# Projections and modulation vectors moved inside two attention blocks of a two-layer transformer stack

## The chip, the cores and the metric

The kernel runs on one core of a Trainium2 chip. The metric is device time in microseconds (us), lower is better. Before the change three runs took 2095.98, 2098.3 and 2098.57 us, the median being 2098.3 us. Products of TensorE (PE) are in fp32 pieces; VectorE is DVE, ScalarE is ACT, GpSimd is POOL, and SP issues most weight transfers.

## The reference, cut to what matters

Input x is 512 tokens by 1024 features. Four blocks follow one another; each begins with an RMS norm that is scaled and shifted by vectors computed from a conditioning row c:

```python
mod = silu(c) @ w_ada[layer] + b_ada[layer]          # three rows of 1024: shift, scale, gate
h = rmsnorm(x, g_pre) * (1 + scale) + shift
# block 1 (even): z = h @ w_in, split into latent q and kv (MLA, 8 heads), SWA q, k, v (8 heads, window 128), gate
o = concat([mla(...), swa_sink(...)]) * silu(z_gate);  x = x + gate * rmsnorm(o @ w_out)
# block 2 (odd): z = h @ w_in, split into dq, dk, dv (4 differential heads), fq, fk, fv, ff (8 forgetting heads), gate
o = concat([diff(...), forgetting(...)]) * silu(z_gate);  x = x + gate * rmsnorm(o @ w_out)
# then a convolution block with an MLP, an HGRN2 block with an MLP, and a last RMS norm
```

All attention is causal (SWA over a band of two blocks), softmax is in fp32, and every product with a weight matrix must keep fp32 accuracy.

## The kernel before, in words

**Products.** Every fp32 operand of a large product is split into a high and a low half of a reduced fp32 type, and `mm3` (L206) issues three TensorE instructions for each pair of 128-row tiles (high by high, low by high, high by low). `wgran` (L210) brings a granule of 512 KB of a weight matrix to a `raw` buffer by SP, casts the high half on ACT (L222) and subtracts to get the low half on DVE or, every `lo_pool`-th time, on POOL (L225). Five `hl` buffers hold granules. `gemm_xs` (L288) takes tokens as the stationary operand: for each of four token blocks it accumulates 8 x 3 products into one PSUM buffer and hands it to an `evac` function. `gemm_ws` (L351) takes the weights as stationary operand and gives transposed results, 512 tokens wide. PSUM tags are `mm`, `sc`, `tp` with two buffers each, `pv` and `tq` with one.

**Attention.** The generators `mla`, `swa`, `diff` and `fox` each have 16 steps (head pairs, or heads, by four query blocks). A step is scores (PE), a masked minimum (DVE, L633), an exponential (ACT, L635), a reciprocal (DVE, L636), a scaling (POOL, L640), transposes of the probabilities (PE, L663), a copy (ACT, L665) and products with V (PE, L682 or L673). Queries and keys of `mla`, `swa` and `diff` go through DRAM: the projection's evac applies the rotary embedding (two DVE operations L619 and L621, one POOL addition L622), ACT issues a store, and `load` reads a head back and transposes it through PSUM tag `tq` (`heads_T`, L646 to L653).

**Weaving.** `weave` (L263) takes one step of an attention generator and then as many units of a `fill` generator as a cost function allows. A unit is one k-step of a 512-wide product group (three products). `behind` ties the fill to the PE instruction of six steps earlier, so fill may run at most about six steps ahead. The source order gives priorities; a planner with a timeline of its own puts each engine's instructions in a fixed order, so an engine's queue runs strictly in that order on the chip.

**Even block.** After the latent projections the kernel runs the SWA queries' projection (columns 672 to 1183, `gemm_x(..., ev_sq)`) and the first gate alone, then the latent up-projections, then weaves `mla` with 52 units of fill and `swa` with 24: gates 1 to 3, SWA keys and values, gates 4, 6, 5, 7.

**Odd block.** The projections dq, dk and dv, each 512 wide, run alone; then comes the small `ff` product, then `diff` woven with 80 units (gates 0 to 5 and fv), then the first pair of `fqk` alone, then `fox` woven with 64 units (three pairs of `fqk`, gates 6 and 7).

**Vectors.** `ada` makes the modulation rows for later blocks. Each row is eight steps, appended to `pend`, and `tick` runs one after a product group. `step` (L531) issues an SP load into one of two `araw` buffers and adds it up with two DVE operations (L540, L542); the last of four sums partitions with eight small products (L548). `step_pe` (L512) does the same by eight small TensorE products (L522) and one DVE addition (L524), one tick after the load. Only the convolution block uses `step_pe` before the change. Even and odd blocks have four rows, 32 steps, each.

Of the kernel before, what the change touches and what calls it, by code (L numbers as in the profile page):

```python
# [16 lines left out]
P = 128  # L17
D = 1024
T = 512
NTB = T // P  # L20
KC = D // P
# [9 lines left out]
C_CH = C_SM + 256  # L31
C_SH = C_CH + 256
# [7 lines left out]
STRICT = 0  # L40
FD = 6
ADA_OFF = 0
W_MLA = 52
ONDVE = (0, 1, 2)
W_FOX = 3
MAIN_OFF = 0
# [13 lines left out]
TV = 0  # L60
TVE = 3
# [3 lines left out]
SQF = 0  # L65
G0 = 2
ADA_LAG = 1
# [45 lines left out]
class K:  # L113
# [174 lines left out]
    def gemm_xs(self, act, w, c0, cw, kc, evac, tag="mm", subs=None):  # L288

        gs = self.wload(w, c0, cw, kc)  # L290
        subs = subs or [(0, cw)]
        for tb in range(NTB):
            outs = []
            for s0, sw in subs:
                ps = self.psum(("mm", "sc")[tb % 2] if len(subs) > 1 else tag)
                for k in range(kc):
                    g, j = gs[k]
                    self.mm3(ps[:, :sw], [a[:, k, tb * P:(tb + 1) * P] for a in act],
                             [g[:, a, j, s0:s0 + sw] for a in range(2)], k == 0, k == kc - 1, TERMS_R)
# [185 lines left out]
    def ada(self, ccol, w, b, c0, kind, g=None):  # L485
# [45 lines left out]
        def step(half, gk):  # L531
            if gk == 0:
                st[half] = self.rp.tile([P, 512], F32, tag="acc", name=self.nm("acc"), bufs=1)
            acc = st[half]
            raw = load(half, gk)
            for k in range(2):
                c = ccol[:, gk * 2 + k:gk * 2 + k + 1]
                eng = nc.gpsimd if half in self.ada_pool else nc.vector
                if gk + k == 0:
                    eng.tensor_scalar(out=acc, in0=raw[:, k], scalar1=c, scalar2=None, op0=ALU.mult)  # L540
                else:
                    eng.scalar_tensor_tensor(out=acc, in0=raw[:, k], scalar=c, in1=acc, op0=ALU.mult, op1=ALU.add)  # L542
# [218 lines left out]
    def even(self, act, gs):  # L761
# [43 lines left out]
            nc.scalar.dma_start(out=sqd[tb * P:(tb + 1) * P, 8:10, :], in_=t.rearrange("p (n d) -> p n d", d=64))  # L805
            nc.scalar.copy(out=SV[:, tb], in_=ps[:, 128:256])

        if TV == 1:
            self.tick_every = TVE
        o = self.otile()  # L810
        if SQF:
            self.run(self.gates(act, w, 1440, o, (0, 1)[:G0]))
        else:
            self.gemm_x(act, w, 672, 512, KC, ev_sq)
        if TV == 2:
            self.tick_every = TVE
        cT = [self.b4() for _ in range(5)]
        for c in range(5):
            ps = self.psum("tp")
# [92 lines left out]
                self.pv_out(o[:, 4 + hd // 2, :], pv)  # L912

        def fill():
            if SQF:
                yield from self.gates(act, w, 1440, o, (0, 1)[G0:])
                yield from self.gemm_xs(act, w, 1184, 256, KC, ev_sk)
                yield from self.gates(act, w, 1440, o, (2,))
                yield from self.gemm_xs(act, w, 672, 512, KC, ev_sq)
                yield from self.gates(act, w, 1440, o, (3, 4, 6, 5, 7))  # L920
                return
            yield from self.gates(act, w, 1440, o, (1, 2, 3))
            yield from self.gemm_xs(act, w, 1184, 256, KC, ev_sk)
            yield from self.gates(act, w, 1440, o, (4, 6, 5, 7))

        self.lo_pool = LOP[0]
        if not SQF:
            self.run(self.gates(act, w, 1440, o, (0,)))
        g = fill()
        self.weave(mla(), 16, g, W_MLA + 16 * SQF)  # L930
        self.weave(swa(), 16, g, (96 - 8 * G0 if SQF else 76) - W_MLA)
        return o


    def odd(self, act):
# [2 lines left out]
        dqk = self.dp.tile([T, 2, 512], F32, name="dqk")  # L938
        lam_init = 0.8 - 0.6 * math.exp(-0.3 * 1)

        def ev_rope(i):
            def e(tb, ps):
                t = self.tmp()[:, :512]
                self.rope(t.rearrange("p (n d) -> p n d", d=64), ps.rearrange("p (n d) -> p n d", d=64), tb, 8, 64, C_CH, C_SH)
                nc.scalar.dma_start(out=dqk[tb * P:(tb + 1) * P, i, :], in_=t)
            return e

        def ev_v(V):
# [17 lines left out]
        sub = self.cp.tile([P, 1], F32, name="sub")  # L966
        nc.vector.tensor_scalar(out=sub, in0=self.vcol("od_subln", 0), scalar1=0.5 * (1.0 - lam_init), scalar2=None, op0=ALU.mult)

        self.gemm_x(act, w, 0, 512, KC, ev_rope(0))
        self.gemm_x(act, w, 512, 512, KC, ev_rope(1))  # L970
        V = []

        def ev_vd(tb, ps):
            V.append(self.work("Vd", [P, 512]))
            nc.scalar.copy(out=V[tb], in_=ps)

        self.gemm_x(act, w, 1024, 512, KC, ev_vd)
        o = self.otile()

        A = self.work("foxA", [P, T], F32R)  # L980
# [91 lines left out]
        V2, qkT = [], {}  # L1072

        def fill():
            yield from self.gates(act, w, 3080, o, range(6))
            yield from self.gemm_xs(act, w, 2560, 512, KC, ev_v(V2))

        self.lo_pool = LOP[1]
        self.weave(diff(), 16, fill(), 80)
        self.run(fqk(0, qkT))  # L1080

        def fill():
            for p in range(1, 4):
                yield from fqk(p, qkT)
                if p > 1:
                    yield from self.gates(act, w, 3080, o, (p + 4,))

        g = fill()
        main = fox(qkT, V2)
        self.weave(main, 16, g, lambda i: min(4 * i, 16) + max(0, min(5 * (i - 4), 40)) + max(0, 2 * (i - 12)))  # L1090
        self.run(g)
        return o

# [547 lines left out]
def build(tc, h, upto=99):  # L1641
    nc = tc.nc
    with ExitStack() as es:
# [17 lines left out]
        def first(i, mixer, act, xsrc, xdst, wout, **bufs):  # L1661
            with tc.tile_pool(name="xp", bufs=1, reuse_waits="tile") as k.xp:
                with k.scope(**bufs):
                    k.tick_every = TO if i else 1000
                    k.ada_pool = AP[i]
                    rows = [k.ada(cc, wa[i], ba[i], 2048, "gatepost", h["g_post"][i])]
                    if i == 0:
                        rows += [k.ada(cc, wa[1], ba[1], 1024, "scale", h["g_pre"][1]),
                                 k.ada(cc, wa[1], ba[1], 0, "shift")]
                    else:  # L1670
                        rows += [k.ada(cc2, wa2[0], ba2[0], 1024, "scale", h["norm1_g_2"][0]),
                                 k.ada(cc2, wa2[0], ba2[0], 0, "shift")]
                        mods[0] = [k.ada(cc2, wa2[0], ba2[0], 2048, "gate")]
                    if G2 == 2 + i:
                        mods["g2"] = k.ada(cc2, wa2[0], ba2[0], 5120, "gate")
                    o = mixer(act)
                    k.flush()
                    k.lo_pool, k.tick_every = 0, 1
                    k.ada_pool = ()
                    if MK & 4:  # L1680
                        k.mark()
                with k.scope(t4=3, rows=3, oT=2, hl2=3):
# [145 lines left out]
```

## Time and profile before

| | before |
|---|---|
| median of three runs | 2098.3 us |
| profiled execution: time / span | 2094.94 / 2093.2 us |
| PE busy | 1956.3 us (93%) |
| weight loads (PEld) busy | 1585.6 us (76%) |
| DVE / ACT / POOL busy | 64% / 41% / 35% |
| mean granted TensorE clock | 0.963 |

The span is the stretch from the first to the last instruction; the profiled execution's own time is 1.7 us longer. A PE that is listed as busy is not PE at its peak: ends of products are modelled, and short gaps disappear. The granted clock is 1.00 at 2.4 GHz and 0.50 at 1.2 GHz. The even block lies at about 30 to 360 us of the span, the odd block at about 360 to 760 us.

### The profile page before, as it was taken

How to read it: one execution, taken by the hardware profiler on the slowest of the kernel's cores; microseconds unless marked ns; L12 is line 12 of the kernel's file. 1: busy time of each engine (PE TensorE's matmuls, PEld its weight loads, DVE VectorE, ACT ScalarE, POOL GpSimd, SP SyncE). 2: the span in 40 equal slices, each digit the busy share in tenths (PEclk: the TensorE clock that was granted, in tenths of full speed). 3: DMA queues.
4: the chain of work that ended last, by engine and by line, in shares of the span. 5: the costliest groups of instructions: out<-in, count | busy, mean ns of one | idle time of the engine just before them, and what ended most of it. 6: DMA issues, size and time to landing. Idle time of an engine off the chain costs nothing.

```text
span 2093.2 us, 32588 instructions
## 1 busy us (share of the span) xinstructions
PE 1956.3 (93%) x12759; PEld 1585.6 (76%) x12759; DVE 1345.0 (64%) x1979; ACT 861.8 (41%) x1461; POOL 733.1 (35%) x660
## 2 busy tenths in 40 slices
PE   7799999798999999879899999999999998999998
PEld 5688668565667787458788989877877778898896
DVE  5356775535545479547987748667786858485673
ACT  4345553133554432143434435343554534353452
POOL 1233334221233333015232331456675544223232
PEclk9999979997999999899999999999999999999999
DMA  8484655277343436832554225453322322242331
GB/s 311 129 230 136 180 166 161 80 164 145 80 97 104 149 117 187 223 99 71 178 178 153 87 75 182 134 152 103 103 83 82 121 83 80 91 131 71 121 102 60
DMA packets 225745, 272.09 MB, mean 130 GB/s; under 512 B 26682, under 2 KB 145689, under 8 KB 225592
## 3 DMA queue, kind: packets, MB, share of 16 engines
q1 hardware_dynamic: 188982, 232.83, 37.8%
q10 hardware_dynamic: 36610, 37.18, 5.9%
q8 instruction: 101, 1.65, 0.3%
q14 instruction: 52, 0.43, 0.1%
HBM read 253.57 MB, written 16.40 MB: 129 GB/s over the span
## 4 chain that ended last, share of the span: by engine, by line
PE 41%; DVE 12%; issue 4%; DMA 4%; POOL 2%; ACT 1%; ACTq 0%; SPq 0%; POOLq 0%; DVEq 0%
PE mm L208 23%; PE mm L1223 4%; PE sc L208 4%; PE sc L1223 3%; PE tp L1223 3%; DVE acc L542 2%; DVE ol L1343 2%; DVE hl L201 1%; DMA ud<-u 1%; DVE hl L225 1%; DMA raw<-in_ada_w_dram 1%; PE pv L208 1%; DVE X L1585 1%; DMA u<-ud 1%; DMA raw<-in_mlp_w_dram 0%
## 5 line engine op out<-in xcount | busy, mean ns | idle before, releaser
L208 PE MATMUL mm<-hTh,hl 128*128 128x512 f32 (+2 forms) x1200 | 375.3, 389 | 3.0 <-DVE V L201 1.5
L222 ACT CAST hl<-raw 128x1024 fp32r<-128x1024 f32 (+2 forms) x219 | 224.4, 1033 | 245.7 <-PE mm L208 142.8
L208 PE MATMUL mm<-hl,hid 128*128 128x512 f32 x1344 | 316.9, 395 | 4.9 <-DVE hid L201 3.3
L225 DVE TENSOR_TENSOR hl<-raw,hl 128x1024 fp32r<-128x1024 f32 (+2 forms) x190 | 251.0, 1331 | 78.3 <-ACT hl L222 77.8
L208 PEld LDWEIGHTS mm<-hl,hid 128*128 128x128 f32 x1344 | 251.9, 188 | 64.7 <-DVE hid L201 4.3
L208 PEld LDWEIGHTS mm<-hTh,hl 128*128 128x128 f32 (+1 forms) x1200 | 221.6, 191 | 51.6 <-issue 3.8
L208 PE MATMUL mm<-hl,hTh 128*128 128x512 f32 (+3 forms) x752 | 223.6, 375 | 26.5 <-DVE t L621 11.0
L208 PE MATMUL mm<-hTl,hl 128*128 128x512 f32 (+2 forms) x600 | 232.8, 388 | 0.1
L1140 POOL TENSOR_TENSOR xr<-xr,t 128x512 f32<-128x512 f32 x56 | 80.3, 1433 | 305.6 <-DVE t L1137 304.2
L208 PEld LDWEIGHTS mm<-hl,hTh 128*128 128x128 f32 x752 | 141.8, 199 | 52.2 <-ACT t L788 8.7
L542 DVE SCALAR_TENSOR_TENSOR acc<-araw,ccol,acc 128x512 f32<-128x512 f32 x154 | 135.0, 876 | 36.3 <-DMA araw<-in_ada_w_dram 24.3
L640 POOL TENSOR_TENSOR s<-s,sm 128x256 f32<-128x256 f32 (+3 forms) x112 | 82.8, 740 | 193.1 <-DVE sm L636 184.9
L200 ACT CAST hl<-raw 128x1024 fp32r<-128x1024 f32 x84 | 86.8, 1048 | 135.9 <-PE mm L208 111.3
L208 PE MATMUL mm<-hl,hTl 128*128 128x512 f32 (+3 forms) x376 | 139.8, 372 | 0.4 <-DVE hTl L458 0.4
L201 DVE TENSOR_TENSOR hl<-raw,hl 128x1024 fp32r<-128x1024 f32 x84 | 131.3, 1578 | 13.6 <-ACT hl L200 12.9
L208 PEld LDWEIGHTS mm<-hTl,hl 128*128 128x128 f32 (+1 forms) x600 | 114.5, 191 | 23.6 <-issue 2.0
L1203 POOL TENSOR_TENSOR raw<-raw,raw 128x1024 f32<-128x1024 f32 x28 | 76.2, 2722 | 144.4 <-DVE rows L1203 95.1
L225 POOL TENSOR_TENSOR hl<-raw,hl 128x1024 fp32r<-128x1024 f32 x29 | 73.1, 2520 | 120.5 <-ACT hl L222 120.5
L635 ACT ACTIVATE s<-s,sm 128x256 f32<-128x256 f32 (+5 forms) x128 | 69.6, 544 | 95.0 <-DVE sm L633 89.4
L1137 DVE TENSOR_TENSOR t<-mm,rows 128x512 f32<-128x512 f32 x56 | 38.5, 687 | 106.8 <-PE mm L208 103.1
L208 PE MATMUL sc<-b,b 64*128 64x256 f32 (+7 forms) x384 | 94.5, 361 | 10.5 <-DVE sm L633 8.2
L1588 POOL TENSOR_TENSOR X<-X,T 128x512 f32<-128x512 f32 x56 | 74.2, 1330 | 50.5 <-ACT op L1548 32.7
(366 smaller groups left out, 3960.4 us busy)
## 6 DMA issues: line engine op xcount, KB each, us to landing
raw<-in_mlp_w_dram SPq DMA_DIRECT2D x128, 512.0 KB
araw<-in_ada_w_dram SPq DMA_DIRECT2D x72, 512.0 KB
raw<-in_hgrn_w_in_dram SPq DMA_DIRECT2D x40, 512.0 KB
araw<-in_w_ada_dram SPq DMA_DIRECT2D x32, 512.0 KB
raw<-in_od_w_in_dram SPq DMA_DIRECT2D x32, 512.0 KB
raw<-in_ada_w_dram SPq DMA_DIRECT2D x24, 512.0 KB
rows<-row SPq DMA_DIRECT2D x16, 512.0 KB
raw<-in_conv_w_in_dram SPq DMA_DIRECT2D x16, 512.0 KB
```

What stands on the lines that cost most here:

```text
L200: nc.scalar.copy(out=hi, in_=src)
L201: nc.vector.tensor_tensor(out=lo, in0=src, in1=hi.bitcast(F32), op=ALU.subtract)
L208: self.nc.tensor.matmul(out, lhsT=lt[a], rhs=rt[b], start=start and n == 0, stop=stop and n == 2)
L222: self.nc.scalar.copy(out=hi, in_=raw[:, :n])
L225: eng.tensor_tensor(out=lo, in0=raw[:, :n], in1=hi.bitcast(F32), op=ALU.subtract)
L542: eng.scalar_tensor_tensor(out=acc, in0=raw[:, k], scalar=c, in1=acc, op0=ALU.mult, op1=ALU.add)
L635: nc.scalar.activation(out=s[:, :m], in_=s[:, :m], func=AF.Exp, scale=-1.0, bias=mn, accum_out=sm)
L640: nc.gpsimd.tensor_tensor(out=p, in0=p, in1=r.to_broadcast([P, n]), op=ALU.mult)
L1140: eng.tensor_tensor(out=xs, in0=xs, in1=t, op=ALU.add)
L1203: eng.tensor_tensor(out=out, in0=x, in1=y, op=f)
L1223: nc.tensor.matmul(ps[:, m * 256:m * 256 + 256], lhsT=ws[n][:, a, k, m * P:m * P + P], rhs=parts[n][b][:, k], start=m + k + t == 0, stop=m ...
L1588: nc.gpsimd.tensor_tensor(out=xk, in0=xk, in1=cap(Tt, 1, [(row - 1, 2), (2, nb), (0, hh)]), op=ALU.mult)
```

## The change

In the even block the SWA queries' projection leaves the front and becomes part of the fill, and so does gate 0; `mla` is woven with 80 units and `swa` with 32, 112 in all (76 before). The 32 vector steps of this block use `step_pe`, through PSUM tag `tq`. In the odd block dq, dk and dv are projected in two halves of 256 columns: heads 0 and 1 before `diff`, through `mm` and `sc` buffers in turn, heads 2 and 3 inside `diff`'s fill. `diff` has 128 units of fill (gate 0, the second halves, gates 1 and 2, fv, gate 3, the first pair of `fqk`), `fox` has 80 at six a step. Everywhere, `step` does its DVE sums one tick after its load.

```diff
-W_MLA = 52
+W_MLA = 80
@@ gemm_xs
-                ps = self.psum(("mm", "sc")[tb % 2] if len(subs) > 1 else tag)
+                ps = self.psum(("mm", "sc")[tb % 2] if len(subs) > 1 or tag == "wide" else tag)
@@ ada, step
             raw = load(half, gk)
+            self.ada_late.append(lambda: sums(half, gk, acc, raw))
+            self.ada_do(ADA_LAG)
+
+        def sums(half, gk, acc, raw):
             for k in range(2):
@@ even
-            self.gemm_x(act, w, 672, 512, KC, ev_sq)
...
-            yield from self.gates(act, w, 1440, o, (1, 2, 3))
+            yield from self.gates(act, w, 1440, o, (0,))
             yield from self.gemm_xs(act, w, 1184, 256, KC, ev_sk)
-            yield from self.gates(act, w, 1440, o, (4, 6, 5, 7))
+            yield from self.gates(act, w, 1440, o, (1, 2))
+            yield from self.gemm_xs(act, w, 672, 512, KC, ev_sq)
+            yield from self.gates(act, w, 1440, o, (3, 4, 6, 5, 7))
-            self.run(self.gates(act, w, 1440, o, (0,)))
-        self.weave(mla(), 16, g, W_MLA + 16 * SQF)
-        self.weave(swa(), 16, g, (96 - 8 * G0 if SQF else 76) - W_MLA)
+        self.weave(mla(), 16, g, W_MLA)
+        self.weave(swa(), 16, g, 112 - W_MLA)
@@ odd
-        self.gemm_x(act, w, 0, 512, KC, ev_rope(0))
-        self.gemm_x(act, w, 512, 512, KC, ev_rope(1))
-        self.gemm_x(act, w, 1024, 512, KC, ev_vd)
+        def dqkv(n):
+            for i in range(2):
+                yield from self.gemm_xs(act, w, 512 * i + 256 * n, 256, KC, ev_rope(i, 256 * n), tag="wide" if n == 0 else "mm")
+            yield from self.gemm_xs(act, w, 1024 + 256 * n, 256, KC, ev_vd(256 * n), tag="wide" if n == 0 else "mm")
+        self.run(dqkv(0))
...
-            yield from self.gates(act, w, 3080, o, range(6))
+            yield from self.gates(act, w, 3080, o, (0,))
+            yield from dqkv(1)
+            yield from self.gates(act, w, 3080, o, (1, 2))
             yield from self.gemm_xs(act, w, 2560, 512, KC, ev_v(V2))
-        self.weave(diff(), 16, fill(), 80)
-        self.run(fqk(0, qkT))
+            yield from self.gates(act, w, 3080, o, (3,))
+            yield from fqk(0, qkT)
             for p in range(1, 4):
                 yield from fqk(p, qkT)
-                if p > 1:
-                    yield from self.gates(act, w, 3080, o, (p + 4,))
+                yield from self.gates(act, w, 3080, o, (p + 3,))
+            yield from self.gates(act, w, 3080, o, (7,))
-        self.weave(main, 16, g, lambda i: min(4 * i, 16) + max(0, min(5 * (i - 4), 40)) + max(0, 2 * (i - 12)))
+        self.weave(diff(), 16, g, lambda i: 8 * i)
+        self.weave(fox(qkT, V2), 16, g, lambda i: 6 * i)
@@ first
+                    k.ada_pe, k.ada_ps = i == 0, "tq"
```

`ev_rope` and `ev_vd` are cut to 256 columns accordingly: twice as many rotary operations, stores and copies, each half as wide.

## Rows read from the trace of the kernel before

**Rows 1.** Windows: us; busy PE, PEld, DVE, ACT, POOL (count); clock, DMA, GB/s.
```profile
145.00:163.00 18.00, 15.49 (x84) 12.59 (x83) 13.85 (x32) 8.24 (x20) 5.56 (x6) 0.82 0.73 224
163.00:280.00 117.00, 114.25 (x776) 85.98 (x775) 84.55 (x234) 62.83 (x173) 42.95 (x75) 1.00 0.50 144
280.00:307.30 27.30, 27.30 (x119) 17.26 (x118) 17.08 (x53) 11.28 (x38) 10.64 (x21) 0.51 0.58 167
...
370.00:463.00 93.00, 79.42 (x332) 60.02 (x332) 41.63 (x61) 24.50 (x30) 23.87 (x15) 0.94 0.54 126
463.00:535.00 72.00, 59.39 (x248) 42.74 (x249) 37.79 (x98) 26.19 (x58) 13.54 (x12) 0.76 0.63 121
535.00:592.00 57.00, 54.84 (x267) 39.08 (x266) 31.63 (x83) 30.94 (x61) 15.19 (x12) 1.00 0.52 106
592.00:682.00 90.00, 89.83 (x477) 64.22 (x478) 44.93 (x123) 41.57 (x99) 32.77 (x35) 0.96 0.32 98
682.00:699.60 17.60, 15.65 (x112) 9.90 (x110) 7.50 (x22) 10.13 (x26) 5.36 (x7) 1.00 0.52 169
699.60:2093.00 1393.40, 1322.36 (x9297) 1104.77 (x9296) 965.61 (x1118) 564.46 (x809) 520.76 (x397) 0.98 0.38 118
```

**Rows 2.** Timeline of PE, 512-wide products: start, length, line, operation, count.
```profile
84.97 0.39 PE L208 MATMUL mm<-hl,hTl 128*128 128x512 f32 x1
...
88.47 0.40 PE L208 MATMUL mm<-hl,hTl 128*128 128x512 f32 x1
88.71 0.51 PE L208 MATMUL sc<-hl,b 128*128 128x384 f32 x2
```

**Rows 3.** Timeline of PE, 256-wide products in latent attention's fill.
```profile
181.11 0.27 PE L208 MATMUL mm<-hl,hTl 128*128 128x256 f32 x1
...
182.53 0.28 PE L208 MATMUL mm<-hl,hTl 128*128 128x256 f32 x1
```

**Rows 4.** Groups of DVE, 145 to 307 us: busy, mean ns, idle before.
```profile
L542 DVE SCALAR_TENSOR_TENSOR acc<-araw,ccol,acc 128x512 f32<-128x512 f32 x56 | 47.4, 847 | 1.6 <-DMA araw<-in_ada_w_dram 1.4
```

**Rows 5.** Timeline of PE, vector products of both kinds.
```profile
803.45 1.08 PE L522 MATMUL tp<-araw,ccol 128*32 128x128 f32 x32
804.46 0.50 PE L208 MATMUL mm<-hTl,hl 128*128 128x512 f32 x1
...
686.86 0.43 PE L548 MATMUL mm<-acc,ones 128*32 128x128 f32 x8
687.22 0.79 PE L208 MATMUL sc<-b,b 64*128 64x384 f32 x3
```

**Rows 6.** Line L524, 760 to 1000 us: ns min/median/max, first and last start.
```profile
L524 DVE TENSOR_TENSOR arow<-tp,arow x16: 271/274/279, 788.9 to 846.3; 128x128 f32<-128x128 f32 x16
```

**Rows 7.** Timeline of PE, last product of the even block's fill.
```profile
273.46 0.39 PE L208 MATMUL mm<-hTh,hl 128*128 128x512 f32 x1
```

**Rows 8.** Waits for buffer araw, 395 to 545 us: us, times; then DVE's timeline, idle in brackets.
```profile
  DMA araw<-in_ada_w_dram: 11.0, 3
...
505.44 0.75 DVE L542 SCALAR_TENSOR_TENSOR acc<-araw,ccol,acc 128x512 f32<-128x512 f32 x1 [3.74 <-DMA araw<-in_ada_w_dram]
```

**Rows 9.** Timeline of PE in differential attention.
```profile
506.51 1.01 PE L208 MATMUL sc<-b,b 64*128 64x256 f32 x3 [3.45 <-DVE sm L633]
```

**Rows 10.** Timeline of all engines, start of the odd block.
```profile
391.48 0.33 ACTq L945 DMA_DIRECT2D dqk<-t  x1
391.92 1.99 ACT L222 CAST hl<-raw 128x1024 fp32r<-128x1024 f32 x2 [11.64 <-POOL t L622]
```

**Rows 11.** Groups of DVE, 360 to 470 us.
```profile
L619 DVE TENSOR_TENSOR ru<-mm,cst 128x512 f32<-128x512 f32 x8 | 5.5, 689 | 9.8 <-PE mm L208 8.6 <-POOL t L622 1.2
```

**Rows 12.** Timeline of PE, last product of the odd block's fill.
```profile
682.69 0.40 PE L208 MATMUL mm<-hTh,hl 128*128 128x512 f32 x1
```

**Rows 13.** Waits: line L522, 760 to 1000 us; then DVE, 1340 to 1640 us.
```profile
  DVE ol L1343: 9.9, 9
...
DVE acc L542 <- DMA raw<-in_ada_w_dram: 19.6, 7, 4.7
```

More of the change, by code (lines that the diff above doesn't have):

```diff
@@ L806, in ev_sk @@
             nc.scalar.copy(out=SV[:, tb], in_=ps[:, 128:256])
-        if TV == 1:
-            self.tick_every = TVE
         o = self.otile()
-        if SQF:
-            self.run(self.gates(act, w, 1440, o, (0, 1)[:G0]))
-        else:
-            self.gemm_x(act, w, 672, 512, KC, ev_sq)
-        if TV == 2:
-            self.tick_every = TVE
         cT = [self.b4() for _ in range(5)]
@@ L914, in fill @@
         def fill():
[L915 to L921, printed above, removed]
-            yield from self.gates(act, w, 1440, o, (1, 2, 3))
+            yield from self.gates(act, w, 1440, o, (0,))
             yield from self.gemm_xs(act, w, 1184, 256, KC, ev_sk)
-            yield from self.gates(act, w, 1440, o, (4, 6, 5, 7))
+            yield from self.gates(act, w, 1440, o, (1, 2))
+            yield from self.gemm_xs(act, w, 672, 512, KC, ev_sq)
+            yield from self.gates(act, w, 1440, o, (3, 4, 6, 5, 7))
         self.lo_pool = LOP[0]
-        if not SQF:
-            self.run(self.gates(act, w, 1440, o, (0,)))
         g = fill()
-        self.weave(mla(), 16, g, W_MLA + 16 * SQF)
-        self.weave(swa(), 16, g, (96 - 8 * G0 if SQF else 76) - W_MLA)
+        self.weave(mla(), 16, g, W_MLA)
+        self.weave(swa(), 16, g, 112 - W_MLA)
         return o
@@ L939, in odd, with ev_rope @@
         lam_init = 0.8 - 0.6 * math.exp(-0.3 * 1)
-        def ev_rope(i):
+        def ev_rope(i, c):
             def e(tb, ps):
-                t = self.tmp()[:, :512]
-                self.rope(t.rearrange("p (n d) -> p n d", d=64), ps.rearrange("p (n d) -> p n d", d=64), tb, 8, 64, C_CH, C_SH)
-                nc.scalar.dma_start(out=dqk[tb * P:(tb + 1) * P, i, :], in_=t)
+                t = self.tmp()[:, :256]
+                self.rope(t.rearrange("p (n d) -> p n d", d=64), ps[:, :256].rearrange("p (n d) -> p n d", d=64), tb, 4, 64, C_CH, C_SH)
+                nc.scalar.dma_start(out=dqk[tb * P:(tb + 1) * P, i, c:c + 256], in_=t)
             return e
@@ L967, in odd, with ev_vd, e @@
         nc.vector.tensor_scalar(out=sub, in0=self.vcol("od_subln", 0), scalar1=0.5 * (1.0 - lam_init), scalar2=None, op0=ALU.mult)
-        self.gemm_x(act, w, 0, 512, KC, ev_rope(0))
-        self.gemm_x(act, w, 512, 512, KC, ev_rope(1))
[L971 to L975, printed above, removed]
-        self.gemm_x(act, w, 1024, 512, KC, ev_vd)
+        V = [self.work("Vd", [P, 512]) for _ in range(NTB)]
+        def ev_vd(c):
+            def e(tb, ps):
+                nc.scalar.copy(out=V[tb][:, c:c + 256], in_=ps[:, :256])
+            return e
+        def dqkv(n):
[3 more added lines that the diff above has]
+        self.run(dqkv(0))
         o = self.otile()
@@ L1074, in fill @@
         def fill():
-            yield from self.gates(act, w, 3080, o, range(6))
+            yield from self.gates(act, w, 3080, o, (0,))
+            yield from dqkv(1)
+            yield from self.gates(act, w, 3080, o, (1, 2))
             yield from self.gemm_xs(act, w, 2560, 512, KC, ev_v(V2))
-        self.lo_pool = LOP[1]
-        self.weave(diff(), 16, fill(), 80)
-        self.run(fqk(0, qkT))
-        def fill():
+            yield from self.gates(act, w, 3080, o, (3,))
+            yield from fqk(0, qkT)
             for p in range(1, 4):
                 yield from fqk(p, qkT)
-                if p > 1:
-                    yield from self.gates(act, w, 3080, o, (p + 4,))
+                yield from self.gates(act, w, 3080, o, (p + 3,))
+            yield from self.gates(act, w, 3080, o, (7,))
+        self.lo_pool = LOP[1]
         g = fill()
-        main = fox(qkT, V2)
-        self.weave(main, 16, g, lambda i: min(4 * i, 16) + max(0, min(5 * (i - 4), 40)) + max(0, 2 * (i - 12)))
+        self.weave(diff(), 16, g, lambda i: 8 * i)
+        self.weave(fox(qkT, V2), 16, g, lambda i: 6 * i)
         self.run(g)
@@ L1679, in first @@
                     k.ada_pool = ()
+                    k.ada_pe = False
                     if MK & 4:
```

## The prediction, as it was put on record

> **What bounds the kernel now.** I read the page's busy times first, then windows by stage, then the timelines of PE and DVE in the stretches that the change touches. The chain of waits was no help, since its listing begins only at the convolution block, behind both attention blocks.
>
> PE is listed as busy for 93% of the span, but that hides two losses: idle time, and busy time at a clock below 1.00. I add them per stretch as (length − PE busy) + PE busy × (1 − clock). In the even block [rows 1] this gives 2.5 + 2.8 = 5.3 us for 145 to 163 us (the beginning of latent attention), 2.8 us for 163 to 280, and 13.4 us for 280 to 307.3, where PE is listed as busy throughout, but at clock 0.51 (all but a moment of it at 1.2 GHz). Sum 21.5 us. In the odd block [rows 1] the front, 370 to 463 us, loses 13.6 + 4.8 = 18.4 us; differential attention loses 12.6 + 14.3 = 26.9 us (463 to 535), 2.2 us (535 to 592) and, with the beginning of forgetting attention, 3.8 us (592 to 682), together 32.9 us; the end of forgetting attention loses 2.0 us. So PE is the bound of both blocks, with about 75 us of it not used. Moving a product from one dense place to another gains nothing; it gains what it fills of these losses.
>
> DVE is not the bound, though it is a link of each step: between 163 and 280 us it is busy for 84.6 of 117 us [rows 1], and 47.4 us of its time from 145 to 307 us are vector sums [rows 4]. PE waits through it where a sum stands in DVE's queue in front of a softmax and its weights have not come: three such waits, 11.0 us in all [rows 8]; behind the one of 3.74 us PE stands for 3.45 us, until a reciprocal in DVE's queue is through [rows 9].
>
> **The even block, part by part.** *SWA queries.* 96 products of 512 columns. Fifteen stand between 84.97 and 88.47 us [rows 2], so one takes 0.233 us at the full clock and the projection 22.4 us. They leave the front and come back as 32 units of fill, net 0 on PE. Their casts, rotary work and stores move with them, under attention in which ACT (62.8 of 117 us) and POOL (43.0) have room [rows 1]. What is late next is the latent up-projection: its first product came at 88.71 us, between products of the SWA queries [rows 2]. From 84 us PE now has little else, since the three granules of that weight and two of the next take all five buffers, and gate 0 comes behind them. Cost 0 to 4.7 us; I take 3, nearer to the row.
>
> *Vectors on TensorE.* 32 steps of eight products. In the convolution block 32 products take 803.45 to 804.46, 1.01 us [rows 5], so the 256 take 8.1 us in such batches. Alone between other work, eight narrow products take 0.36 us [rows 5], which gives 32 × 0.36 = 11.5 us. The eight groups of partition sums go, 8 × 0.36 = 2.9 us. So +5.2 to +8.6 us on PE; I take +7, since ticks come singly here. DVE loses 47.4 us of sums [rows 4] and gains 32 additions of 0.274 us [rows 6], 8.8 us. That is 38.6 us less on an engine that is not the bound, worth only what comes next. The price of a product that waits for `tq` is the second rival.
>
> *Beginning of latent attention.* DVE is busy for 13.9 of the 18 us in which PE loses 5.3 [rows 1]. With the sums gone I take back 3; the bounds are 0 and 5.3.
>
> *End of SWA.* The fill's last product starts at 273.46 us [rows 7], 33.8 us before the end. After the 52 units of latent attention, 20 of the 72 real units were left, at 1.5 a step: they were used up, as the source counts, at step 13.3. Now 32 units at 2 a step last to step 16. That covers 2.7 steps more; a step without fill takes about 4 us (27.3 us hold 53 DVE operations, some eight a step, so 6.5 steps), so 11 of the 33.8 us and about a third of the 13.4 us: −4.4. The bounds are 0, if the planner puts the fill as far ahead as before relative to its end, and −13.4.
>
> Sum for the even block: 3 + 7 − 3 − 4.4 = **+2.6 us**. Its order by itself gains nothing that its vectors don't cost.
>
> **The odd block, part by part.** *Halves.* 288 products of 512 columns become 576 of 256. From 181.11 to 182.53 us there are twelve 256-wide ones [rows 3], 0.1183 us each: 68.2 us against 67.2, +1.0. Each brings its own weight load, and the row's pitch has it in it. The Trainium skill (TensorE: Matmul & The Clock Gate, LDWEIGHTS (loading the stationary operand)) speaks against the halves: a load takes its columns divided by 1.2 GHz, 107 ns for 128. By that page's figure 288 more loads would add 31 us, an estimate, if nothing hid them; the row says that the products do hide them.
>
> Rotary operations double in number at half the width. A DVE one took 0.689 us for 512 columns [rows 11]; in halves the sixteen pairs cost between nothing more and, at full price each, 11 us more of DVE in 90 us. DVE is busy for under half of the front and 37.8 of 72 us behind it [rows 1], so this is hidden; without that cover it would delay a store, not PE, since a half of `diff` needs only its own heads. ACT's stores rise by eight issues of 0.33 us [rows 10], behind which its casts stand in the same queue; 2.6 us, hidden by the four granules on hand.
>
> *The stall in the front.* A rotary addition on POOL is late, ACT's store at 391.48 us waits for it, and two casts wait behind that store; ACT has sat 11.64 us [rows 10]. The constants that POOL and DVE compute ahead of it don't change, so I keep this loss: 0.
>
> *Differential attention.* 33.7 us of projection move from before it into its fill, with the first `fqk` pair; gates 4 and 5 go to `fox`. Fill per step rises from 5 units, 3.5 us, to 8 units, 5.6 us. A softmax that is 3 to 4 us late now finds that much more queued ahead of the product that needs it. The lag of one tick also takes a sum whose load has just been issued out of the softmax's way. It doesn't help a burst of ticks: there are still two `araw` buffers, each held a tick longer. Of the 32.9 us lost here I take back 20: the 11 us of waits and the clock that falls after them (14.3 us), less a fifth. The bounds are 0 and 32.9.
>
> *Forgetting attention.* 80 units at 6 a step end at step 13.3, where 64 were spread to step 16. Before, the last fill came at 682.69 us [rows 12], with 17 us left, in which 2.0 us were lost at the full clock [rows 1]. Now about 18 us more have no fill. By that row +2; if the clock falls there as at the end of SWA, 0.49 × 18 = +9. I take +3.
>
> Sum for the odd block: 1 − 20 + 3 = **−16 us**.
>
> **The lag elsewhere.** DVE waits for vector loads for 19.6 us in the HGRN block [rows 13], but behind the odd block PE is idle for 71 of 1393 us at clock 0.98 [rows 1], in four blocks of work. There the loads share the four `raw` buffers with the weights, and the lag holds one longer. Bounds −10 and +3; I take −2.
>
> **Sum.** 2.6 − 16 − 2 = −15.4 us, from the profiled execution's 2094.9 us to 2079.5. That execution lies 3.4 us below the median of the three runs, so the forecast against the median is **2083 us**. The likeliest case's own range is 2068 to 2094.
>
> **Rivals.** *The waits stay (2100 us).* The engines' queues run in order: a product that waits for a late softmax blocks the fill behind it, however much there is. The planner may have put the fill so far ahead that it is gone when the wait comes. Then differential attention returns only 5 us, the lag nothing, and the sum is 2.6 + 1 − 5 + 3 = +1.6. For it: PE had fill to the end of `diff` before and stood all the same [rows 9]. Against it: the worst stretch had only 5 units a step.
>
> *The one `tq` buffer (2117 us, slower).* In the even block 21 groups of transposes (by `heads_T`, two for each of 8 heads and five for SWA) and now 32 product groups share a single PSUM buffer, each emptied by DVE, the transposes by ACT and DVE. A product that finds it full stands at the head of PE's queue. In the convolution block, with two buffers, vector products waited 9.9 us in nine waits for DVE [rows 13], 1.1 us each. At that price for each of the 32 it is 35 us: −15.4 + 35 = +19.6. It decides from 15.4 / 32 = 0.5 us for each product. For it: DVE is still the link that empties. Against it: DVE has 38.6 us less to do. The Trainium skill (Perfetto Trace Analysis, Optimizing Tensor Performance) asks that independent product groups rotate through PSUM banks so that emptying one overlaps the next; these don't. No row of before shows products of this kind in `tq`.
>
> *All of the losses are filled (2055 us).* Even: −13.4 − 5.3 + 5.2 = −13.5; odd: 1 − 32.9 + 2 = −29.9; lag 0, in the middle of its bounds: −43 us. For it: the losses are real and the fill is there. Against it: the last steps always run without fill.
>
> *The change doesn't do what it says:* the planner's order could leave the second halves or the SWA queries where they were; then the time is that of the first rival, and it is counted there.
>
> **How the numbers follow.** Forecast 0.52; waits stay 0.20; `tq` 0.16; all filled 0.12. About 0.2%, 4.2 us, is what a measurement can tell from no change. The forecast's case and the last are faster; of the first rival I count 0.05 as faster, 0.11 as same, 0.04 as slower. Faster 0.69, same 0.11, slower 0.20. The range reaches from the last rival to part of the `tq` case: 2058 to 2110.
>
> **What would show it.** In the changed profile: DVE sums gone before 307 us and L522 products on `tq`; 256-wide pitch 0.118 us; differential attention at clock near 1.00 with under 15 us lost; DVE waits on `araw` in it under 5 us; a fill-less end of SWA of about 23 us; a longer one in forgetting attention; the casts' long wait for POOL in the front still there. The prediction is wrong if PE waits for `tq` by more than 16 us, or if the odd block is not at least 10 us shorter.

## The result, and the profile after

The change makes the kernel slower: its median is 2129.7 us against 2097.1 us of before. The ratio that the record gives for the two series is 1.014, 95% interval 1.0117 to 1.0164, or 29 us of 2100; the medians alone are 32.6 us apart. The forecast was 2083 us. The execution of the trace took 2132.4 us, the slowest of four, 37.5 us above the traced one of before; sums of the traces below come to that figure.

The windows of the kernel after, with the columns of [rows 1]:

```profile
124.00:163.00 39.00, 37.13 (x224) 30.65 (x224) 16.41 (x48) 17.56 (x41) 11.21 (x14) 0.90 0.33 90
163.00:235.00 72.00, 69.11 (x512) 51.13 (x511) 31.79 (x84) 27.09 (x62) 20.68 (x21) 0.98 0.51 153
235.00:275.00 40.00, 31.26 (x287) 20.99 (x284) 15.00 (x56) 13.96 (x40) 9.32 (x22) 0.79 0.55 159
275.00:320.00 45.00, 45.00 (x317) 29.31 (x316) 18.00 (x68) 20.15 (x62) 13.88 (x37) 0.96 0.35 105
320.00:346.00 26.00, 21.66 (x170) 13.22 (x168) 11.27 (x38) 9.97 (x32) 5.94 (x14) 0.82 0.58 156
...
410.00:478.00 68.00, 53.24 (x368) 47.44 (x367) 32.44 (x62) 17.33 (x25) 18.15 (x16) 0.89 0.51 123
478.00:540.00 62.00, 57.76 (x397) 49.73 (x398) 44.26 (x109) 27.19 (x60) 22.35 (x21) 0.94 0.65 159
540.00:610.60 70.60, 70.60 (x351) 51.85 (x349) 44.30 (x99) 37.20 (x71) 19.49 (x15) 1.00 0.74 121
610.60:734.80 124.20, 119.88 (x632) 82.40 (x632) 50.70 (x137) 54.07 (x125) 40.61 (x42) 1.00 0.37 101
734.80:2130.00 1395.20, 1324.88 (x9296) 1104.55 (x9295) 971.88 (x1118) 564.17 (x809) 526.88 (x397) 0.98 0.38 118
```

Three stretches tell where the time went. In the even block the last SWA product starts at 345.4 us (before 307.2): +38.2, although latent attention begins 25 us earlier (first transposes at 120.1, before 145.1). The odd block, from there to forgetting attention's last product, takes 389.0 us (392.2): −3.2. What lies behind, to the end of the span, takes 1396.2 us (1393.8).

Lost TensorE time, added as in the prediction: the even rows give 5.6 + 4.3 + 15.3 + 1.8 + 8.2 = 35.2 us, against 21.5 of [rows 1]. The worst is new: from 235 to 275 us the fill of latent attention is used up, SWA's hasn't begun, and the clock is at 0.79. Not one fill product starts between 234.5 and 275.3 us; before, the longest such gap between latent attention and SWA was 17.7 us. Differential attention loses 7.7 us (29.1 without the beginning of forgetting attention), as hoped; the front (410 to 478) loses 20.6.

VectorE is less busy, as forecast (31.8 of 72 us at 163 to 235), and yet latent attention is slower. Its waits and ScalarE's there, 120 to 346 us (waiting line, releaser, us, times, longest), show the two users of `tq`, the vector products and the transposes:

```profile
DVE arow L524 <- PE tq L522: 22.7, 22, 3.6
...
ACT b L203 <- PE tq L654: 19.9, 9, 6.1
ACT b L200 <- PE tq L654: 10.0, 5, 4.3
```

L654 is before's L650, the transposes of queries and keys; ScalarE waited for them for 9.9 us before. How far they fall behind shows on that line alone, on PE up to the last product of latent attention, before and then after (count; ns min/median/max; first and last start):

```profile
L650 PE MATMUL tq<-cst,t x84: 270/272/421, 145.1 to 242.0; 128*96 128x128 f32 x64, 128*128 128x128 f32 x20
```

```profile
L654 PE MATMUL tq<-cst,t x64: 270/273/449, 120.1 to 237.1; 128*96 128x128 f32 x64
```

Before, all 84 transposes are issued by then, the twenty for SWA among them; after, not one of these twenty. SWA's first product with its weights came 1 us behind latent attention's last before (247.3, 246.2), and comes 14 us behind it after (272.5, 258.0).

### The profile page after: what moved, and what is told of

It reads as the page before. It is cut to its first block, busy times and chain, and to the rows that moved or that the text cites. A ratio compares the mean times of both kernels' runs of the same rounds, so it can differ in the third digit from the quotient of the medians.

```text
span 2130.6 us, 34054 instructions
## 1 busy us (share of the span) xinstructions
PE 1981.5 (93%) x13495; PEld 1609.7 (76%) x13495; DVE 1317.3 (62%) x1951; ACT 863.2 (41%) x1465; POOL 744.2 (35%) x672
## 5 line engine op out<-in xcount | busy, mean ns | idle before, releaser
L222 ACT CAST hl<-raw 128x1024 fp32r<-128x1024 f32 (+3 forms) x219 | 224.2, 1033 | 228.8 <-PE mm L208 114.9
L225 DVE TENSOR_TENSOR hl<-raw,hl 128x1024 fp32r<-128x1024 f32 (+3 forms) x186 | 247.2, 1337 | 63.8 <-ACT hl L222 63.1
L208 PE MATMUL mm<-hl,hTh 128*128 128x256 f32 (+3 forms) x848 | 220.3, 342 | 28.9 <-DVE t L625 20.3
L208 PEld LDWEIGHTS mm<-hl,hTh 128*128 128x128 f32 x848 | 153.0, 202 | 46.1 <-DVE t L625 12.6
L644 POOL TENSOR_TENSOR s<-s,sm 128x256 f32<-128x256 f32 (+3 forms) x112 | 77.5, 692 | 210.3 <-DVE sm L640 199.6
L208 PE MATMUL mm<-hl,hTl 128*128 128x256 f32 (+3 forms) x424 | 143.5, 338 | 0.3 <-DVE hTl L458 0.3
L1197 POOL TENSOR_TENSOR raw<-raw,raw 128x1024 f32<-128x1024 f32 x28 | 76.7, 2739 | 145.1 <-DVE rows L1197 90.5
L225 POOL TENSOR_TENSOR hl<-raw,hl 128x1024 fp32r<-128x1024 f32 x33 | 83.0, 2516 | 84.7 <-ACT hl L222 84.7
L546 DVE SCALAR_TENSOR_TENSOR acc<-araw,ccol,acc 128x512 f32<-128x512 f32 x98 | 86.7, 885 | 29.6 <-DMA araw<-in_ada_w_dram 23.0
L1582 POOL TENSOR_TENSOR X<-X,T 128x512 f32<-128x512 f32 x56 | 78.5, 1407 | 59.7 <-ACT op L1542 46.7
```

Of the source, the lines that this page charges most:

```text
L208: self.nc.tensor.matmul(out, lhsT=lt[a], rhs=rt[b], start=start and n == 0, stop=stop and n == 2)
L222: self.nc.scalar.copy(out=hi, in_=raw[:, :n])
L225: eng.tensor_tensor(out=lo, in0=raw[:, :n], in1=hi.bitcast(F32), op=ALU.subtract)
L644: nc.gpsimd.tensor_tensor(out=p, in0=p, in1=r.to_broadcast([P, n]), op=ALU.mult)
L1197: eng.tensor_tensor(out=out, in0=x, in1=y, op=f)
L1582: nc.gpsimd.tensor_tensor(out=xk, in0=xk, in1=cap(Tt, 1, [(row - 1, 2), (2, nb), (0, hh)]), op=ALU.mult)
```

## The experiments

Each ran against the kernel before on one chip, in five rounds; "by the runs" is the distance of the recorded ratio from 1, times 2100 us, and the brackets behind a ratio are its 95% interval. Two things are read with each time: where the blocks end in the one trace that each run has, and whether the planner, which orders the whole program, left the order of untouched code alone.

It often didn't. Behind the last product of forgetting attention TensorE has 2808 lines in before (equal neighbours drawn together). None of them is out of place in e8 and e11, one or two in e1, e2, e5 and e15, 17 to 33 in e3, e6, e7, e9, e10, e12 and e16. In the changed kernel, e4, e13 and e14 it is 42 to 84, but there the lag changes this code itself. In the odd block, 776 lines, e8 and e11 differ from before by two lines at most and e5, e6 and e7 by up to eight; e1, e2, e9, e10 and e15 differ by 43 to 58, though their edits don't touch that block. Two pairs have the same order of TensorE, VectorE, ScalarE and POOL: e2 and e15 from SWA's end on, e9 and e10 in the whole program. The last two are 2.7 us apart by the runs, so a distance of that size tells nothing.

**The four parts alone.** e1 sets before's even block to TensorE; e2 takes only the order, e3 only `odd`, e4 only the lag.

```diff
+                    k.ada_pe, k.ada_ps = i == 0, "tq"      # e1
-W_MLA = 52                                                 # e2, with the new even()
+W_MLA = 80
```

> The kernel before with one part of the change: in the first attention block the modulation vectors are summed on TensorE (in `tq`), everything else as before. Theory A (the products are the cost: a step of eight takes 0.57 us, so 32 steps less 3.1 us of partition sums make 15 us more of a TensorE that is the bound): +12 to +22 us, with SWA's end later by that much. Theory B (the new order is the cost, the products only fill gaps): 0 to +7 us. Theory C (only the two together cost, since the products burst where the new order has no fill): under +8 us here and under +8 in the run of the order alone.

> The kernel before with only the SWA query projection moved into the fill of the latent attention (80 units there, 32 in SWA), vectors on VectorE as before. Theory A: +5 to +12 us, what the stretch without fill between the two attentions (235 to 275 us in the changed kernel) loses beyond what the vector products put there. Theory B: +20 to +35 us, nearly the whole of the even block's 38 us. Theory C: under +8 us.

> The kernel before with only the second attention block changed: heads 0 and 1 projected first in 256 columns, heads 2 and 3 as fill. Of the changed kernel's trace I read -4 us for this block (-23 us of lost TensorE time in differential attention, given back by +6 us of occupied time in more switches and about +14 us of losses in the front). If these are the odd part's own, this run gives -2 to -8 us. If the front's losses came from the even block's end or the lag (another order of arrival at the block), it gives -10 to -20 us, as predicted for it.

> The kernel before with only the lag: each vector sum on VectorE is put one tick behind its load. The two traces show the stretch behind both attentions equal within 2.2 us (1393.6 and 1395.8), so by them the lag is worth -2 to +4 us; if it were what lifts differential attention to the full clock, it would give -8 us or more by itself.

Measured: vectors 1.0187 (1.016 to 1.0214), +39 us; order 0.9965 (0.995 to 0.9981), −7; odd 1.0045 (1.0028 to 1.0062), +9; lag 1.0006 (0.999 to 1.0022), nothing. Theories B and C fall; theory A's +12 to +22 is too small by half. The order's gain doesn't arise in the even block: in e2's trace SWA ends 2.3 us later than before (309.5 and 307.2), and the odd block, whose code is before's, is 8.1 us shorter (384.1 and 392.2). That is the planner's other order there. Behind both blocks this one trace takes 5.0 us more, so it shows 0.8 of the 7 us.

**Products or buffer.** Against e1, e5 leaves out four of a step's eight products; e6 and e9 put all of them into `tp` and `mm`; e15 does both, halves in `mm`.

```diff
-                for k in range(2):
+                n = 1 if self.ada_half else 2              # e5, e15: 1 in the even block
+                for k in range(n):
-                    k.ada_pe, k.ada_ps = i == 0, "tq"
+                    k.ada_pe, k.ada_ps = i == 0, "tp"      # e6; "mm" in e9, e15
```

> As the run of the vectors alone, but each vector step issues only the four products of its first 128 rows (the other four are left out, and with them half of each sum): loads, buffers, additions and the number of steps stay. Beside before, the vectors alone cost 39 us by the clock of the runs, 33 us in the even block. Theory A1 (TensorE's time for the products is the cost, at 0.57 us a step at the full clock, 1.01 us at half): about half goes, +16 to +24 us. Theory C1 (the wait for the one `tq` buffer and the queue behind it is the cost, whatever the products' number): +30 to +40 us. Theory D1 (SWA and latent attention lose VectorE's sums as cover and the clock falls, with the products a small part): +28 to +36 us.

> As the run of the vectors alone, but the products go to `tp` (two buffers, shared with the transposes of the softmax weights) and not to `tq` (one, shared with the transposes of queries and keys). Theory C1 (one `tq` buffer): the cost falls from +39 us to under +20. Theory A1: within 8 us of +39, since the same products are issued.

> The vectors alone (before's order), with the products in `mm` (two buffers, shared with the fill) and not in `tq` (one, shared with the transposes of queries and keys). With half the products the cost stayed at 37 us, so it isn't TensorE's time; in `tp` it fell to 27 us. Theory C1 (the transposes of the next heads wait for the one `tq` buffer behind the products; at the end of latent attention 16 of 21 groups of them had been issued, before 21): the cost falls to +8 to +20 us, since only fill waits now. Theory F (VectorE's addition of a product stands at the head of its queue until TensorE comes to the product, 28.9 us in 21 waits in the even block, and softmax waits behind it): it stays at +25 to +40 us.

> Vectors alone, in `mm`, with only the products of the first 128 rows of each step (half of each sum is left out). The vectors in `mm` cost 14 us; 32 steps of 0.57 us less 3.1 us of partition sums are 15 us of TensorE. If that is what is left (theory A1, once the `tq` wait is gone), half the products cost 5 to 8 us. If what is left is the path through VectorE and `mm`, 12 us or more stay.

Measured: half the products in `tq` 1.0179 (1.0148 to 1.021), +37.6: nothing saved. In `tp` 1.0131 (1.0093 to 1.0169), +27.5. In `mm` 1.0065 (1.0045 to 1.0084), +13.6. Halves in `mm` 1.0053 (1.0035 to 1.0071), +11. So the same halved products cost some 27 us less in `mm` than in `tq` (e5 and e15). Not all of that is the buffer's: SWA ends 16.0 us earlier (341.6 and 325.6), the odd block is shorter by another 13.9 (396.9 and 383.0), and there e15 has e2's order, which is 8.1 us shorter than before's without any such products. With whole steps (e1 and e9) SWA ends 5.7 us earlier (340.5 and 334.8), though the runs are 26 us apart.

What the traces do show of `tq` is the stretch without fill between latent attention and SWA: 43.4 us in e1 and 40.8 in e5, as in the changed kernel (40.8), but 23.3 in e6 and none over 10 us in e9 and e15. Of the products' own time the runs don't settle the size (e9 less e15: 2.5 us, no more than e9 and e10 differ). In `mm` SWA ends 9.2 us earlier with half of them, which is half of 32 × 0.57 us; in `tq` it ends no earlier (e1 and e5).

Theory F (VectorE's additions block softmax) was to be told apart by putting each addition a tick later:

```diff
+                if not self.ada_defer:
+                    return add()
+                self.ada_adds.append(add)          # done at the next tick
```

> As the run with the products in `mm`, but each addition on VectorE is put one tick behind its products. Theory F: VectorE's waits for the products nearly go, and the time falls by 8 to 25 us beside the run with `mm`. Theory C1: within 5 us of the run with `mm`.

It measured 1.0078 (1.0056 to 1.01) and tells nothing: the planner issued the additions where they had been, in e9's order line for line. VectorE's wait for the products, 146 to 320 us, is to the tenth e9's (there line L524):

```profile
DVE arow L526 <- PE mm L522: 26.3, 23, 4.2
```

In the same stretch e1 waits less, 22.4 us in 15, and isn't cheaper than e9, so these waits don't make the difference between the two buffers. What they cost in either is not shown: F stays untested.

**Vectors on TensorE in SWA alone.**

```diff
         def swa():
+            self.ada_pe = True    # from the next half vector on
```

> The new order of the SWA queries, with vectors on TensorE only for those halves of a vector that begin in SWA (about three of eight, 12 steps), on VectorE in the latent attention. In the run of the vectors alone the stretch from the first transposes to SWA's first product grew by 32 us, SWA itself not at all (60 us in both) though it took 16 of the steps. If a step costs by its place (theory E: in SWA it fills time that the half clock would have lost), this run is at the order alone (0.9965 of before), within 5 us, or below it. If a step costs the same anywhere (theory A1), it is +10 to +18 us above the order alone.

1.0061 (1.004 to 1.0082), 20 us above e2. The trace has SWA's end at 311.1 us, 1.6 behind e2's 309.5: in the block the twelve steps cost next to nothing, as theory E said. The traces lie 15.5 us apart; 9.7 us of that arise in the odd block, which has before's order in e7 and not e2's, and 4.2 behind. So this run settles nothing of the total.

**The front of the odd block.** In the changed kernel TensorE stands there (410 to 478 us lies in the window), and POOL's timeline says why:

```profile
PE mm L208 <- DVE t L625: 11.4, 1, 11.4
DVE ru L623 <- POOL t L626: 19.1, 5, 16.0
```

```profile
424.92 0.74 POOL L626 TENSOR_TENSOR t<-t,ru 128x256 f32<-128x256 f32 x1 [2.46 <-issue]
434.49 0.28 POOL L955 PARTITION_BROADCAST nlam<-sm  x1 [8.83 <-issue]
441.71 0.71 POOL L626 TENSOR_TENSOR t<-t,ru 128x256 f32<-128x256 f32 x1 [6.93 <-issue]
```

A broadcast of 0.28 us keeps POOL from 425.7 to 441.7 us. Behind it stands the rotary addition, VectorE's next rotary product waits up to 16.0 us for POOL to be done with the `ru` buffer, and TensorE wants the PSUM buffer that VectorE empties. Before, POOL stood there too:

```profile
382.89 0.28 POOL L965 PARTITION_BROADCAST nlam<-sm  x1 [6.10 <-issue]
390.20 1.25 POOL L622 TENSOR_TENSOR t<-t,ru 128x512 f32<-128x512 f32 x1 [7.02 <-issue]
```

The Trainium skill (GPSIMD Engine Reference, Instruction dispatch) gives some 6 us of unseen code loading for the first call of a freshly loaded POOL routine; the 6.1 us for which POOL stands ahead of this broadcast in the kernel before are near it, the 8.8 us of the changed kernel are more. That it is code loading no row shows. e8 replaces both broadcasts of the kernel before by products on TensorE, e11 does so in the new order of the even block, e12 adds the odd block's change, e16 its halves without the move.

```diff
-        nc.gpsimd.partition_broadcast(nlam, nl[:1])
+        nc.tensor.matmul(ps[:, :n], lhsT=self.ones[:1], rhs=row, start=True, stop=True)
+        nc.vector.tensor_copy(out=out, in_=ps[:, :n])
         self.run(dqkv(0))
+        self.run(dqkv(1))          # e16, with before's fill and weave
```

> The kernel before with its two broadcasts of a row to all partitions (the sinks, in the even block's front, and the factor of differential attention, in the odd block's) taken from POOL to a product with a column of ones on TensorE. In before's trace POOL does nothing for 6.1 us ahead of each and 6.7 to 7.0 us behind it, and rotary additions and row factors stand in its queue meanwhile; TensorE has a gap of 7.30 us at 385.73 us. If the broadcast is what holds the front: -5 to -14 us. If the front is held by something else (weights, row factors), 0 to -3 us.

> The new order of the SWA queries (0.9965 of before by itself) with the two broadcasts on TensorE (0.9926 by itself), vectors on VectorE, odd block as before. If the two don't touch, 0.989 (-23 us), a span of about 2075 us. If the sinks' broadcast was hidden or worth only in before's order, 0.992 to 0.995.

> As the run of order and broadcasts, with the odd block's change added (heads 0 and 1 first). Alone, the odd change cost 9 us; its trace shows TensorE stand for 11.91 us at 397.13 us behind the broadcast, where before stood for 7.30. If the broadcast was what took its gain: 4 to 12 us below the run of order and broadcasts. If the shorter front has too little work to cover the chain from the block's input to the first softmax, whatever the broadcast: equal to it or slower by up to 10 us.

> New order and broadcasts on TensorE (0.9917 of before), with the odd block's projections cut into halves of 256 columns but all of them ahead of differential attention, and before's fill behind them: the halves without the move. With halves and move the ratio was 0.9974, 12 us more. Theory H (the halves: more evictions, rotary operations, stores and ticks): 8 to 15 us above 0.9917. Theory M (the move: a front too short to cover its chain, and fill that costs switches): within 4 us of 0.9917.

Measured: e8 0.9926 (0.99 to 0.9953), −15.6 us; e11 0.9917 (0.9902 to 0.9933), 2083.0 us, the lowest time here, below e2, but not to be told from e8. The two parts don't add up, and the orders say why: e11 has e8's order in the odd block, not e2's, and takes as long there (384.7 and 384.8 us), so e2's gain isn't in it. e12 0.9974 (0.9959 to 0.9989), 12 above e11, though TensorE's waits for VectorE's rotary work in the front fell to 2.7 us (12.7 in e3). e16 1.0026 (1.0009 to 1.0043), 11 above e12 and 23 above e11, more than either theory gave: the halves without the move are worse (odd block 398.2 us, e12 380.0), so the move itself brings something.

Since e12's trace has the odd block 5 us shorter (380.0 against 384.7) and the unchanged rest longer, e17 and e18 cut e11 and e12 behind the odd block.

```diff
-def build(tc, h, upto=99):
+def build(tc, h, upto=2):
```

> Order and broadcasts, as the run at 0.9917 of before, but the program ends behind the second block's output projection (its result is written out; everything behind is left out). By that kernel's trace the rows of forgetting attention end at 688 us, so some 760 us. It is the base for the next run; no theory differs on it.

> The same cut kernel with the odd block's change. The whole kernels differ by 12 us by their runs, while by one trace of each the odd block got 5 us shorter and the unchanged rest 11 us longer. If the odd block itself costs: 8 to 14 us above the cut base. If it gains and the loss arises behind it (clock or queues of the unchanged rest): 0 to 8 us below the cut base.

751.7 us (all runs 749.6 to 755.4) and 741.9 us (741.2 to 744.5): the odd change makes the blocks 9.9 us faster. Windows from the end of the even block into the first steps of forgetting attention, e17 and then e18:

```profile
300.00:430.00 130.00, 124.56 (x527) 99.05 (x527) 68.53 (x93) 39.41 (x64) 41.02 (x42) 0.93 0.43 123
430.00:610.00 180.00, 158.33 (x745) 113.14 (x743) 94.54 (x238) 85.48 (x172) 50.95 (x41) 0.91 0.49 119
```

```profile
300.00:430.00 130.00, 109.14 (x651) 93.00 (x650) 70.58 (x111) 41.77 (x73) 45.47 (x47) 0.91 0.56 128
430.00:610.00 180.00, 175.68 (x992) 134.94 (x992) 111.45 (x264) 88.07 (x181) 60.93 (x53) 0.99 0.49 134
```

The second window is the gain: 175.7 us busy at 0.99, where 158.3 at 0.91 was; the first shows the front thinner. Behind the cut the whole kernels differ the other way, 2083.0 − 751.7 = 1331.3 against 2095.5 − 741.9 = 1353.6 us, for the same instructions in another order. A stretch of that code, e11 and e12:

```profile
980.00:1003.00 23.00, 18.98 (x136) 17.89 (x135) 23.00 (x19) 14.27 (x19) 7.62 (x3) 0.85 0.42 133
```

```profile
983.00:1011.00 28.00, 20.17 (x139) 19.34 (x138) 27.96 (x25) 15.57 (x21) 8.92 (x3) 0.82 0.42 133
```

VectorE is busy throughout in both, with 25 operations in its way where there were 19. That the new order is the cause of all 22 us is not shown: by the whole kernels' traces the part behind the blocks differs by 11.2 us (1393.2 and 1404.4) and the blocks gain 2.8, no run kept one order under both fronts, and the planner orders the cut kernels' blocks otherwise (e17 differs from e11 in some 150 of TensorE's 780 lines of the odd block).

**In the changed kernel itself.** e13 puts its vectors into `mm`, e14 back on VectorE (`k.ada_pe` stays False).

> The changed kernel with the vector products of its even block in `mm` instead of `tq`; nothing else. Alone, that took the vectors' cost from 39 to 14 us. Theory C1 (shared `tq` buffer): 15 to 30 us less than the changed kernel, a ratio to before of 1.000 to 1.008. If in the new order the cost has another root (fill gone between latent attention and SWA): 0 to -8 us, 1.010 to 1.016.

> The changed kernel with its vectors back on VectorE (order, odd block and lag stay). By the single parts: order -7, odd +9, lag +2, so +4 us, a ratio of 1.002; the vectors would then be some 26 us of the change's 30. If the parts interact, it is off this by more than 8 us.

e13: 1.0089 (1.0071 to 1.0108), 11 us less than the changed kernel by the runs, less than C1's 15 to 30. In the trace SWA ends at 320.0 instead of 345.4 us, 25.4 earlier, and what is lost again lies behind (odd block +2.4, the rest +10.8, with 35 to 38 lines out of place). In the block's source nothing but the buffer differs, and the losses account for it:

```profile
240.00:280.00 40.00, 32.81 (x278) 21.96 (x271) 13.92 (x56) 13.88 (x41) 10.15 (x23) 0.74 0.50 147
```

```profile
120.00:320.00 200.00, 191.04 (x1504) 137.34 (x1502) 92.88 (x293) 89.63 (x237) 59.38 (x106) 0.99 0.52 157
240.00:280.00 40.00, 38.47 (x270) 25.25 (x269) 15.85 (x58) 16.22 (x48) 9.74 (x26) 1.00 0.40 130
```

The first line is the changed kernel's, the other two e13's. From 120 to 320 us e13 loses 9.0 + 1.9 = 10.9 us, where the changed kernel loses 35.2 from 124 to 346 us; no gap in its fill is over 10 us. ScalarE's waits for the transposes fall from 29.9 to 13.3 us. That SWA's transposes come late is not in itself the loss: in e13, too, sixteen of them are behind latent attention's last product (235.3).

e14: 1.003 (1.0012 to 1.0049), 2105.2 us: without the vectors on TensorE, 23 of the 29 us are gone, and what is left is near the sum of the other parts (+3). Its traced execution is the slowest of its twelve (2116.0 us); SWA ends at 313.5 us there, so in the block the vectors cost 31.9 us in `tq` and 6.5 in `mm`.

## Why the prediction was wrong

**The failing step: "Vectors on TensorE", taken at +7, bounds +5.2 to +8.6,** with nothing for the wait on `tq`. They cost 39 us alone and 23 in the change by the runs, 31.9 in the even block by the traces. Two things were wrong. The products were mis-sized: the 32 rows in 1.01 us [rows 5] are two steps, not four, since a step's eight products are listed as sixteen instructions. The other bound, 32 × 0.36, has the same error: a partition sum is four products, listed as eight, and not the eight that stand ahead of the prediction. Timeline of PE, one step at the full clock in the changed kernel, then one at half in e1:

```profile
161.06 0.64 PE L522 MATMUL tq<-araw,ccol 128*32 128x128 f32 x16
161.63 0.66 PE L667 MATMUL tp<-cst,s 128*128 128x128 f32 x4
```

```profile
246.56 1.08 PE L522 MATMUL tq<-araw,ccol 128*32 128x128 f32 x16
247.57 0.69 PE L208 MATMUL sc<-b,b 96*128 96x128 f32 x2
```

To the next product's start that is 0.57 us, 1.01 at half clock: 32 × 0.57 − 2.9 = +15 us of TensorE's time. How much of it the kernel pays is not settled: 6.5 us by e13 and e14, 18.4 by e9 and e15, if half of them cost 9.2.

The larger part is the buffer: in the changed kernel 25.4 us of the block go with `tq` alone (e13), 11 by the runs. That is the second rival (2117 us, chance 0.16). Its kind was right, its place wrong: TensorE's products hardly stood in front of a full `tq` (3.6 us), so the prediction's own sign, over 16 us of such waits, did not come; its other sign did, the odd block being 3 us shorter and not 10. With two users of one `tq`, latent attention falls back (last product at 258.0 us, in e13 at 235.3), its fill is used up before its steps, and 40 us run bare at a low clock. All three traces with the whole block's products in `tq` have this gap, and no trace with `mm` has it. That late transposes are what holds latent attention back is argued, not shown: ScalarE's waits for them fall by half from the changed kernel to e13, but are 16.9 us in e1 and 17.7 in e9. And no run tells the sharing from the single buffer, since `mm` has two buffers and other users.

**The even block's losses,** forecast to shrink by 3 + 4.4 us, grew by 13.7. The end of SWA went as forecast: 22.4 us without fill (33.8 before, forecast 23), and 8.2 us lost where 13.4 were. The beginning of latent attention did not: it loses 5.1 us in its first 18 (5.3). The new gap, 15.3 us, stood in no term. The order without the vectors, 3 − 3 − 4.4 = −4.4 by these terms, gains 7 by e2's runs; but the trace has that gain in the odd block, through an order that nobody chose, so the agreement is luck.

**Differential attention:** −20 of the losses, traced −21 (29.1 to 7.7), with VectorE's waits for `araw` at 4.9 us (forecast under 5; 17.0 before, 460 to 592 us): right, and hardly by the lag, since e3 has 5.2 without it and the lag alone (e4) leaves 11.1. **The front's stall,** "I keep this loss: 0", grew from 6.9 to 11.4 us, and the front behind is thinner; so the block got 3 us, not 16. With the broadcasts off POOL the cut blocks get 9.9. **Forgetting attention,** +3: its fill ends 14.1 us before its last product (16.7 before), not the forecast's 35, it loses 4.3 us in all (5.7 before), and the clock doesn't fall. **The lag,** −2: nothing that can be measured.

## What to carry to other kernels

Before work moves to an engine with room, ask through which buffer its result leaves and who else waits for that buffer. A buffer of one that two kinds of work share need not show as a wait of the moved work for it: here the trace showed it as a stretch without fill at a low clock. Where one planner orders the whole program, compare the instruction order of the untouched code before you credit or blame an edit by the total: here the one stretch in which a part gained was one that its edit didn't touch. Compare runs whose order is the same, read the cost where the edited block ends, or cut the program behind the edit. A stall that "stays" has to be priced again when the work that covered it is moved away.

## What the runs showed of the hardware

An fp32 product of 128 columns into 32 rows is listed as two instructions (512 for the 256 of the even block's steps), sixteen in 0.57 us at the full clock and in 1.01 at half. A POOL broadcast listed at 0.28 us takes POOL out for 13 us before and 16 us after the change; the two of this kernel are worth 15.6 us of its time by the runs (e8).
